# The two gates and the two output projections of a hybrid decoder layer: weights in pairs of K blocks and column blocks, and seven products of block sums for three of eight gate pairs

## The chip, the core and the metric

The kernel runs on one NeuronCore of a Trainium2 chip. Its engines work side by side, each through its own queue in order: TensorE (PE, with its weight loads shown as PEld), VectorE (DVE), ScalarE (ACT), GpSimd (POOL) and SyncE (SP); DMA queues move data between HBM, the on-chip memory SBUF and DRAM scratch. TensorE writes its sums into PSUM, here used as eight banks of 128 x 512 numbers. The metric is the device time of one execution in microseconds, the median of several runs. The changed kernel is timed against the one before on the same chip.

## The reference

One layer on 256 tokens of width 2048, in float32:

```python
h = rmsnorm(x, pre_norm_g)
q_a, c_kv, k_rope, z_mla, c_in, b_gate, c_gate, z_conv, g_mla, g_conv = split(h @ w_in)
attn = causal_mla_attention(...) * silu(z_mla)      # 16 heads, from q_a, c_kv, k_rope
y_mla = attn @ w_o_mla                              # 2048 x 2048
u = c_gate * c_in
conv = sum(conv_w[k] * u_pad[:, k:k + s] for k in range(3))
y_conv = (b_gate * conv * silu(z_conv)) @ w_o_conv  # 2048 x 2048
merged = sigmoid(g_mla) * y_mla + sigmoid(g_conv) * y_conv
out = x + rmsnorm(merged @ w_out, post_norm_g)
```

`g_mla` and `g_conv` are two more products of 256 x 2048 by 2048 x 2048, of the normalised input with columns of `w_in`. These four products and the sum that joins them are called the merged stage here; behind it comes the product with `w_out`.

## The kernel before

**Number format.** Every matrix product is made from three matmuls (`product`, L227): each float32 operand is split into a high and a low part of a format that TensorE takes at full pace, and high x high, high x low and low x high are added up in PSUM. For weights the split is made on the chip: ScalarE copies the float32 piece into the high part (`whi`, L245), and VectorE subtracts it from the piece to get the low part (`wlo`, L246), both in `split_act`. For activations both parts stand side by side in tiles whose names end in `_both`: `x_both` (the input, 16 blocks of K by 256 tokens), `at_both` (the gated attention), `cv_both` (the gated convolution) and `m_both` (the merged result).

**Weights.** All weights come in units of 128 x 2048 numbers (1 MB), in the order of a list called `plan`. `take(i)` hands out unit i; ahead of that, `ahead` has started the loads of the next units (three buffers `raw`) and issued the splits up to unit i + 1. The split halves, of 1024 columns, live in rings of five buffers, `whi` and `wlo`: a half can be split as soon as the matmuls that read the half five places earlier are done. A unit feeds 24 matmuls.

**Stages.** The products for the latents come first, then 16 rounds of attention heads mixed with the convolution's products, then the merged stage, then the output. In the merged stage before, an outer loop runs over four blocks of 512 columns (c), an inner one over the four products (n): gate of the attention, gate of the convolution, attention's projection, convolution's projection. `tokens(c, n, cols)` (L934) makes one of them: four units of four K blocks each, for two groups of 128 tokens (t), into two PSUM banks of the ring "mm" (four banks). The gates go through the sigmoid (L970) into 512-wide tiles `sg`, the projections are multiplied in (L980, L985), the two are added (L986), turned block by block through DRAM (`turned`, L316: VectorE transposes blocks of 32, GpSimd issues four stores and, behind their landing, one load), and split into `m_both` by `features` (L953) some units later. During the first block of columns the attention and the convolution are split into `at_both` and `cv_both` (L924, L929).

**Banks.** PSUM has rings of banks by name: "mm" (four), "cv" (two, for the convolution's products in the attention stage), "st" (one, scores of a head) and "o" (one, values of a head). The values of the last head are read from "o" by L395 on ScalarE and L396 on VectorE.

**Memory.** SBUF is handed out in pools that are opened and closed. The attention stage's pool is `bp`; at its close (L913) the pool of `at_both` and `cv_both` is opened where it was (L914). Among `bp`'s buffers are `mv` and `cw`, through which the last pieces of the convolution are turned at the very end of the attention stage. At L1009 `main` is closed and the pool `op` opened, with the residual `xr`, the weighted output `og` and the post-norm gain `gb` (L1016), which `out_block` (L1019) reads for each output block.

**Order.** The instructions of each engine are put in order by a scheduler that plans with its own estimates of durations: of the instructions that are ready it takes the one that stands first in the program. TensorE's matmuls, and whatever is marked `keep_in_program_order`, stay in program order.

Of the kernel before, what the change touches and what calls it, by code (L numbers as in the profile page):

```python
# [41 lines left out]
XW = S + R  # L42

# [39 lines left out]
def tile_layer(ctx: ExitStack, tc: tile.TileContext, xw, w0, xb, x, pos, pvec, post_g, wc, wz, wcv, wkr, wqk, wqr, wv, cwr, wsq, out):  # L83
# [84 lines left out]
    def split_unit(i):  # L168
# [12 lines left out]
        if i <= u_qa[-1]:  # L181
# [8 lines left out]
            return  # L190
        for h in range(0, w, HALF):
            n = min(HALF, w - h)
            if u_out[3, 0] <= i < u_out[3, 3]:
                hi, lo = (op.tile([P, HALF], F32R, name=f"w{o}{i}_{h}") for o in ("hi", "lo"))
# [5 lines left out]
        splits[i] = parts  # L200

# [11 lines left out]
    def take(i):  # L213
        ahead(i)
        parts = splits.pop(i)

# [700 lines left out]
    dp = main.enter_context(tc.tile_pool(name="dp", bufs=1))  # L917

    def split_turned(src, both, c, t):
        ks, ts = slice(4 * c, 4 * c + 4), slice(t * P, (t + 1) * P)  # L920
        lo = slice(t * P + S, (t + 1) * P + S)
        split_act(quarters(both[:, ks, ts]), quarters(both[:, ks, lo]), by_rows(src, 4), True)

    def split_branch(i):  # L924

        for t in range(NT):
            split_turned(at_t[:, i, t, :], at_both, i, t)

    def split_channels(i):  # L929

        j, t = divmod(i, NT)
        split_turned(cv_t[:, j, t, :], cv_both, j, t)

    def tokens(c, n, cols):  # L934

        pss = [bank(f"sq{c}_{n}_{t}") for t in range(NT)]
        for kk in range(4):
            w = take(u_d[c][n][kk])
            if c == 0 and n == 0:
                split_branch(kk)  # L940
# [253 lines left out]
```

## Time and profile before

| what | value |
|---|---|
| time, median of 3 runs | 1034.92 us (1034.39 to 1035.58) |
| span of the profiled execution | 1033.7 us |
| what lies around the span, against the median | 1.2 us |
| TensorE matmuls, busy | 1027.6 us, 4684 matmuls |
| VectorE busy | 683.5 us, 957 instructions |
| ScalarE busy | 527.4 us, 735 instructions |
| merged stage, first to last matmul | 590.5 to 938.7 us |
| output product | 938.7 to about 1027 us |

The profiled execution has no device time of its own beside its span, so sums are made against the span and carried to the median. Engines overlap, so their busy times don't add up to the span. A matmul's shown duration overlaps those of its neighbours; the pace of a row of them is the stretch divided by their count. In the rows shown below, the first number of a timeline row is its start in us from the span's start, the second its duration; "x8" counts instructions; a bracket gives the idle time in front and what ended it. In rows of groups the numbers behind the bar are busy time in us, mean duration in ns, and the idle time in front.

### The profile page before, as it was taken

How to read it: one execution, taken by the hardware profiler on the slowest of the kernel's cores; microseconds unless marked ns; L12 is line 12 of the kernel's file. 1: busy time of each engine (PE TensorE's matmuls, PEld its weight loads, DVE VectorE, ACT ScalarE, POOL GpSimd, SP SyncE). 2: the span in 40 equal slices, each digit the busy share in tenths (PEclk: the TensorE clock that was granted, in tenths of full speed). 3: DMA queues.
4: the chain of work that ended last, by engine and by line, in shares of the span. 5: the costliest groups of instructions: out<-in, count | busy, mean ns of one | idle time of the engine just before them, and what ended most of it. 6: DMA issues, size and time to landing. Idle time of an engine off the chain costs nothing.

```text
span 1033.7 us, 12740 instructions
## 1 busy us (share of the span) xinstructions
PE 1027.6 (99%) x4684; PEld 856.7 (83%) x4684; DVE 683.5 (66%) x957; ACT 527.4 (51%) x735; POOL 178.7 (17%) x344
## 2 busy tenths in 40 slices
PE   9999999999999999999999999999999999999998
PEld 8888888888888888888888888888888888888886
DVE  7588787787777777777777785564455455455562
ACT  7665545655456454564555565344434444443451
POOL 4540421104300223112133120020010001002000
PEclk9999999999999999999999999999999999999999
DMA  9775865668665676857686765565565557558642
GB/s 353 278 261 204 276 221 219 211 197 288 215 250 193 223 265 209 275 187 242 228 270 226 265 217 199 204 226 185 200 219 209 188 201 241 183 188 337 228 163 81
DMA packets 44526, 233.25 MB, mean 226 GB/s; under 512 B 7952, under 2 KB 10512, under 8 KB 21552
## 3 DMA queue, kind: packets, MB, share of 16 engines
q1 hardware_dynamic: 32400, 199.67, 54.6%
q0 software_dynamic: 11632, 29.48, 8.8%
q10 hardware_dynamic: 432, 3.29, 0.8%
q8 instruction: 36, 0.59, 0.2%
q14 instruction: 26, 0.21, 0.1%
HBM read 215.66 MB, written 12.58 MB: 221 GB/s over the span
## 4 chain that ended last, share of the span: by engine, by line
PE 96%; DMA 2%; ACT 1%; DVE 0%; issue 0%; DVEq 0%; SPq 0%
PE cv L88 34%; PE sq L88 34%; PE out L88 8%; PE z L88 6%; PE qa L88 2%; PE vv L88 2%; PE kn L88 2%; PE qn L88 2%; PE ckv L88 2%; PE sc L88 1%; PE qr L88 1%; PE o L88 1%; DMA raw<-wz_dram 1%; DMA at_f<-far_qa 1%; DMA at_f<-far_ckv 0%
## 5 line engine op out<-in xcount | busy, mean ns | idle before, releaser
L246 DVE TENSOR_TENSOR wlo<-raw,whi 128x1024 fp32r<-128x1024 f32 (+1 forms) x370 | 440.5, 1196 | 279.8 <-ACT whi L245 268.4
L245 ACT ACTIVATE whi<-raw 128x1024 fp32r<-128x1024 f32 (+1 forms) x372 | 382.4, 1035 | 401.6 <-PE sq L88 180.5
L88 PE MATMUL cv<-whi,x_both 128*128 128x512 f32 x1024 | 319.8, 389 | 0.0
L88 PEld LDWEIGHTS cv<-whi,x_both 128*128 128x128 f32 x1024 | 192.3, 188 | 39.4
L88 PE MATMUL cv<-wlo,x_both 128*128 128x512 f32 x512 | 199.6, 390 | 0.0
L88 PE MATMUL sq<-whi,x_both 128*128 128x512 f32 x512 | 158.3, 389 | 0.0
L88 PEld LDWEIGHTS sq<-whi,x_both 128*128 128x128 f32 x512 | 96.1, 188 | 19.9
L88 PEld LDWEIGHTS cv<-wlo,x_both 128*128 128x128 f32 x512 | 96.1, 188 | 19.5 <-DVE wlo L246 0.2
L88 PE MATMUL sq<-wlo,x_both 128*128 128x512 f32 x256 | 99.6, 389 | 0.0
L88 PE MATMUL z<-whi,x_both 128*128 128x512 f32 x256 | 80.0, 389 | 0.0
L88 PE MATMUL sq<-whi,at_both 128*128 128x512 f32 x256 | 79.5, 389 | 0.0
L88 PE MATMUL sq<-whi,cv_both 128*128 128x512 f32 x256 | 79.5, 389 | 0.0
L88 PE MATMUL out<-whi,m_both 128*128 128x512 f32 x256 | 78.9, 389 | 0.0
L328 POOL DMA_DIRECT2D far<-sg x32 | 17.5, 553 | 313.0 <-DVE sg L320 238.4
L328 POOL DMA_DIRECT2D far<-via x64 | 35.1, 556 | 177.9 <-DVE via L320 177.9
L88 PEld LDWEIGHTS sq<-wlo,x_both 128*128 128x128 f32 x256 | 48.0, 188 | 10.0
L88 PEld LDWEIGHTS sq<-whi,at_both 128*128 128x128 f32 x256 | 48.0, 188 | 9.9
L88 PEld LDWEIGHTS out<-whi,m_both 128*128 128x128 f32 x256 | 48.0, 188 | 9.9
L88 PEld LDWEIGHTS sq<-whi,cv_both 128*128 128x128 f32 x256 | 48.0, 188 | 9.9
L88 PEld LDWEIGHTS z<-whi,x_both 128*128 128x128 f32 x256 | 48.1, 188 | 9.9
L88 PE MATMUL z<-wlo,x_both 128*128 128x512 f32 x128 | 49.8, 389 | 0.0
L88 PE MATMUL sq<-wlo,at_both 128*128 128x512 f32 x128 | 49.8, 389 | 0.0
(216 smaller groups left out, 1128.9 us busy)
## 6 DMA issues: line engine op xcount, KB each, us to landing
raw<-wsq_dram SPq DMA_DIRECT2D x80, 1024.0 KB, 4.8
raw<-wcv_dram SPq DMA_DIRECT2D x64, 1024.0 KB, 5.6
raw<-wz_dram SPq DMA_DIRECT2D x16, 1024.0 KB, 4.9
raw<-wqk_dram SPq DMA_DIRECT2D x8, 1024.0 KB, 6.0
cw<-cwr_dram POOLq DMA_DIRECT2D x24, 256.0 KB, 6.0
raw<-wc_dram SPq DMA_DIRECT2D x4, 1024.0 KB, 10.5
raw<-wv_dram SPq DMA_DIRECT2D x4, 1024.0 KB, 4.8
far<-via POOLq DMA_DIRECT2D x64, 48.0 KB, 4.1
```

The lines of the kernel that those rows point to most:

```text
L88: return tc.keep_in_program_order(nc.tensor.matmul(*a, **kw))
L245: a = nc.scalar.activation(hi, src, AF.Copy)
L246: b = nc.vector.tensor_tensor(lo, src, hi.bitcast(F32), op=ALU.subtract)
L328: tc.keep_in_program_order(queue.dma_start(out=f[i], in_=m))
```

## The change

The weights of the four products are now packed in pairs: a unit holds two blocks of K (128 rows each) by two blocks of columns (512 each), that is four blocks b11, b22, b21, b12, for pair k of eight and column block c of two. The loops run over the product n outside and c inside, so a block (n, c) has eight units and four accumulated outputs (two groups of tokens t by two blocks of columns j), instead of four units and two outputs.

For the two gates (n < 2), three of the eight pairs (`FAST`: 0, 3, 5) are not multiplied as eight blocks, but with seven: VectorE forms sums of the four blocks of weights (`split_seven`: three sums, then three and a half splits where two were), once per kernel sums of the four blocks of activations (`mixed`, kept in `mix`), and the seven products go into seven banks (`p1`, `q5`, `q7`, `q6`, `p2`, `q3`, `q4`). The other five pairs add their plain products onto four banks (`p2`, `q3`, `q4`, `d22`), so a block of a gate uses all eight banks: the four "mm", "st", "o" and both "cv". `first_sums` (after the last of the three units) and `last_sums` (at the end of the block) join them into the gate. In the first block the order of the pairs is 1, 2, 0, 4, 3, 6, 5, 7.

The tiles change place: the sums, `mix` and the gates in their full width (`gate`) lie in a new pool `sp`, opened at the close of `bp`; the split attention goes into `x_both`, block by block, behind the last gate's matmuls, the split convolution into the freed `at_f` and `x_both`, the merged result into `x_both`. The merged result is turned in two lots of four pieces instead of four lots of two. The output product begins with the first two units of three column blocks, and splits the last merged pieces ahead of its sixth unit instead of its third; `op` is opened there, after the close of `sp`.

```diff
+PAIRS = KD // 2
+FAST = (0, 3, 5)
...
-    u_d = [[[add(wsq[n, c, k]) for k in range(4)] for n in range(4)] for c in range(4)]
-
-    out_order = [(c, k) for c in range(2) for k in range(3)] + [(0, 3), (1, 3)]
-    out_order += [(c, k) for c in (2, 3) for k in range(4)]
-    u_out = {ck: add(wsq[4, ck[0], ck[1]]) for ck in out_order}
+    pair_order = {(n, c): list(range(PAIRS)) for n in range(4) for c in range(2)}
+    pair_order[0, 0] = [1, 2, 0, 4, 3, 6, 5, 7]
+    u_d, seven = {}, set()
+    for n in range(4):
+        for c in range(2):
+            for k in pair_order[n, c]:
+                u_d[n, c, k] = add(wd[n, c, k])
+                if n < 2 and k in FAST:
+                    seven.add(u_d[n, c, k])
+
+    out_order = [(c, k) for c in range(3) for k in range(2)] + [(c, k) for c in range(3) for k in (2, 3)]
+    out_order += [(3, k) for k in range(4)]
+    u_out = {ck: add(wo[ck[0], ck[1]]) for ck in out_order}
 
...
+        if i in seven:
+            splits[i] = split_seven(i, t)
+            return
...
+    def split_seven(i, t):
+        hi, hi2 = (wpool.tile([P, HALF], F32R, name=f"whi{i}_{j}", tag="whi", bufs=5) for j in range(2))
+        lo, lo2 = (wpool.tile([P, HALF], F32R, name=f"wlo{i}_{j}", tag="wlo", bufs=5) for j in range(2))
+        ta, tb = (sp.tile([P, HALF], F32, name=f"ts{i}_{j}", tag="ts", bufs=2) for j in range(2))
+        ha, hb = (sp.tile([P, HALF], F32R, name=f"th{i}_{j}", tag="th", bufs=2) for j in range(2))
+        la, lb = (sp.tile([P, HALF], F32R, name=f"tl{i}_{j}", tag="tl", bufs=2) for j in range(2))
+        plus = lambda o, a, b: nc.vector.tensor_tensor(o, a, b, op=ALU.add)
+        two = lambda a: a.rearrange("p (j c) -> p j c", j=2)
+        plus(two(ta[:, :]), two(t[:, :HALF]), t[:, 3 * R :].unsqueeze(1).to_broadcast([P, 2, R]))
+        plus(tb[:, :R], ta[:, :R], t[:, R:HALF])
+        plus(tb[:, R:], tb[:, :R], t[:, HALF : 3 * R])
+        split_act(hi[:, :], lo[:, :], t[:, :HALF])
+        split_act(hi2[:, :R], lo2[:, :R], t[:, HALF : 3 * R])
+        split_act(ha[:, :], la[:, :], ta[:, :])
+        split_act(hb[:, :], lb[:, :], tb[:, :])
+        f = lambda a: (a[:, :R], a[:, R:])
+        (b11, b22), (t1, t3), (t2, t4) = (list(zip(f(h), f(l))) for h, l in ((hi, lo), (ha, la), (hb, lb)))
+        return {"b11": b11, "b22": b22, "b21": (hi2[:, :R], lo2[:, :R]), "t1": t1, "t2": t2, "t3": t3, "t4": t4}
 
...
-    fstack = main.enter_context(ExitStack())
-    fp = fstack.enter_context(tc.tile_pool(name="fp", bufs=1, side="right"))
-    at_f = fp.tile([P, H, S], F32, name="at_f")
-    cv_f = fp.tile([P, KD, S], F32, name="cv_f")
+    cstack, astack = (main.enter_context(ExitStack()) for _ in range(2))
+    cv_pool = cstack.enter_context(tc.tile_pool(name="cv_pool", bufs=1, side="right"))
+    cv_f = cv_pool.tile([P, KD, S], F32, name="cv_f")
+    at_pool = astack.enter_context(tc.tile_pool(name="at_pool", bufs=1, side="right"))
+    at_f = at_pool.tile([P, H, S], F32, name="at_f")
...
     bstack.close()
-    cp = main.enter_context(tc.tile_pool(name="cp", bufs=1))
-    at_both = cp.tile([P, H, 2 * S], F32R, name="at_both")
-    cv_both = cp.tile([P, KD, 2 * S], F32R, name="cv_both")
...
-    def tokens(c, n, cols):
-
-        pss = [bank(f"sq{c}_{n}_{t}") for t in range(NT)]
...
+    spool = ctx.enter_context(ExitStack())
+    sp = spool.enter_context(tc.tile_pool(name="sp", bufs=1))
+    gate = [[sp.tile([P, D], F32, name=f"g{n}_{t}") for t in range(NT)] for n in range(2)]
+    mix = {k: sp.tile([P, 2, 4 * P], F32R, name=f"mix{k}") for k in FAST}
+
...
+    def mixed(k):
+        tmp = sp.tile([P, R], F32, name=f"xr{k}", tag="ev", bufs=2)
+        f = tmp[:, :].rearrange("p (j s) -> p j s", j=2)
+        ks = slice(2 * k, 2 * k + 2)
+        nc.vector.tensor_tensor(f, x_both[:, ks, :S].bitcast(F32), x_both[:, ks, S:].bitcast(F32), op=ALU.add)
+        raw = sp.tile([P, R], F32, name=f"xm{k}", tag="ev", bufs=2)
+        a11, a21, a12, a22 = (f[:, j, t * P : (t + 1) * P] for j in range(2) for t in range(2))
+        m7, m5, m6, m3 = (raw[:, j * P : (j + 1) * P] for j in range(4))
+        minus = lambda o, a, b: nc.vector.tensor_tensor(o, a, b, op=ALU.subtract)
+        minus(m7, a21, a11)
+        minus(m5, a21, a22)
+        minus(m6, a11, m5)
+        minus(m3, a12, m6)
+        split_act(mix[k][:, 0, :], mix[k][:, 1, :], raw[:, :])
+
...
+    def fast_block(n, c, part, outs, between):
+        q = {name: bank(f"{name}_{n}{c}") for name in ("p1", "q5", "q7", "q6")}
+        q["p2"] = bank(f"p2_{n}{c}", tag="st", bufs=1)
+        q["q3"] = bank(f"q3_{n}{c}", tag="o", bufs=1)
+        q["q4"], q["d22"] = (bank(f"{name}_{n}{c}", tag="cv", bufs=2) for name in ("q4", "d22"))
+        order = pair_order[n, c]
+        calls = []
+        for k in order:
+            if k in FAST:
+                for name, a, b in (
+                    ("p1", part(2 * k, 0), "b11"), ("q5", mix_part(k, 1), "t1"), ("q7", mix_part(k, 0), "t3"),
+                    ("q6", mix_part(k, 2), "t2"), ("p2", part(2 * k + 1, 0), "b21"), ("q3", mix_part(k, 3), "b22"),
+                    ("q4", part(2 * k + 1, 1), "t4"),
+                ):
+                    calls.append((k, name, a, b))
+            else:
+                for name, t, j in (("p2", 0, 0), ("q3", 0, 1), ("q4", 1, 0), ("d22", 1, 1)):
+                    for i in range(2):
+                        calls.append((k, name, part(2 * k + i, t), {(0, 0): 0, (1, 1): 1, (1, 0): 2, (0, 1): 3}[i, j]))
+        firsts, lasts = {}, {}
+        for at, (k, name, a, b) in enumerate(calls):
+            firsts.setdefault(name, at)
+            lasts[name] = at
+        t_a, t_b = (sp.tile([P, R], F32, name=f"ev{i}_{n}{c}", tag="ev", bufs=2)[:, :] for i in range(2))
+        (o11, o12), (o21, o22) = outs
+        tt = lambda o, a, b, op=ALU.add: nc.vector.tensor_tensor(o, a, b, op=op)
+
+        def first_sums():
+            nc.scalar.activation(t_a, q["p1"][:, :], AF.Copy)
+            tt(t_b, q["q6"][:, :], t_a, ALU.subtract)
+            tt(o12, q["q5"][:, :], t_b)
+            tt(o21, q["q7"][:, :], t_b)
+            tt(o22, q["q5"][:, :], o21)
+
+        def last_sums():
+            tt(o11, q["p2"][:, :], t_a)
+            tt(o12, q["q3"][:, :], o12)
+            tt(o21, q["q4"][:, :], o21, ALU.subtract)
+            tt(o22, q["d22"][:, :], o22)
+
+        at = 0
+        for i, k in enumerate(order):
+            w = take(u_d[n, c, k])
+            if i == order.index(max(FAST)) + 1:
+                first_sums()
+            between(i)
+            while at < len(calls) and calls[at][0] == k:
+                _, name, a, b = calls[at]
+                product(q[name][:, :], a, w[b] if k in FAST else w(b, R), firsts[name] == at, lasts[name] == at)
+                at += 1
+        last_sums()
+
...
+    for n in range(2):
+        for c in range(2):
+
+            def between(i):
+                if n == c == 0 and i < 2:
+                    for k in FAST[i : i + 1] if i == 0 else FAST[1:]:
+                        mixed(k)
+                if n == c == 1 and i in (2, 4, 6):
+                    split_group(at_place, at_t, i // 2 - 1)
+
+            outs = [[gate[n][t][:, columns(c, j)] for j in range(2)] for t in range(NT)]
+            fast_block(n, c, x_part, outs, between)
             for t in range(NT):
+                for o in outs[t]:
+                    nc.scalar.activation(o, o, AF.Sigmoid, scale=r_col[:, t : t + 1])
+    def between(c, i):
+        if (c, i) == (0, 1):
+            split_group(at_place, at_t, 3)
+        elif (c, i) == (0, 3):
+            astack.close()
+            cv_first["area"] = cv_stack.enter_context(tc.tile_pool(name="cv_first", bufs=1, side="right")).tile(
+                [P, KD // 2, 2 * S], F32R, name="cv_first"
+            )
+        if (c, i) in ((0, 4), (0, 6), (1, 3), (1, 5)):
+            split_group(cv_place, cv_t, {(0, 4): 0, (0, 6): 1, (1, 3): 2, (1, 5): 3}[c, i])
+
+    for c in range(2):
+        q = plain_block(2, c, x_part, lambda i: between(c, i))
+        for (t, j), ps in q.items():
+            g = gate[0][t][:, columns(c, j)]
+            nc.vector.tensor_tensor(g, ps[:, :], g, op=ALU.mult)
+    for c in range(2):
+        q = plain_block(3, c, cv_part, lambda i: features(i - 4) if c and i in (4, 5) else None)
         steps = []
+        for (t, j), ps in q.items():
+            m, y = (gate[i][t][:, columns(c, j)] for i in range(2))
+            nc.vector.tensor_tensor(y, ps[:, :], y, op=ALU.mult)
+            nc.vector.tensor_tensor(m, m, y, op=ALU.add)
+            steps.append((turned(m, y, 4), m))
+            steps[-1][0][0]()
+        for (_, come), m in steps:
+            come(m)
+
...
+    for i, (c, kk) in enumerate(out_order[:6]):
         w = take(u_out[c, kk])
-        if i == 2:
-            features(3, waiting, m_both)
+        if i == 5:
+            for j in (2, 3):
+                features(j)
         out_products(pss[c], w, kk)
-    main.close()
-
+    spool.close()
+    cv_stack.close()
+    cstack.close()
+    op_w = ctx.enter_context(tc.tile_pool(name="op_w", bufs=1, side="right"))
```

`plain_block` is the same loop for the two projections, with eight products per unit into four banks ("mm" for c = 0; "st", "o", "cv", "cv" for c = 1).

More of the change, by code (lines that the diff above doesn't have):

```diff
@@ new lines, in plain_block @@
+    def plain_block(n, c, part, between):
+        tags = ("mm",) * 4 if c == 0 else ("st", "o", "cv", "cv")
+        q = {
+            (t, j): bank(f"sq{n}{c}_{t}{j}", tag=tag, bufs={"mm": 4, "cv": 2}.get(tag, 1))
+            for (t, j), tag in zip(((0, 0), (0, 1), (1, 0), (1, 1)), tags)
+        }
+        order = pair_order[n, c]
+        for at, k in enumerate(order):
+            w = take(u_d[n, c, k])
+            between(at)
+            for (t, j), ps in q.items():
+                for i in range(2):
+                    b = w({(0, 0): 0, (1, 1): 1, (1, 0): 2, (0, 1): 3}[i, j], R)
+                    product(ps[:, :], part(2 * k + i, t), b, at == i == 0, at == PAIRS - 1 and i == 1)
+        return q
@@ L1082, in finish_by_two @@
         store(t, 1024, 1280, o[:, 512:])
-    for c, kk in out_order[3:6]:
-        out_products(pss[c], take(u_out[c, kk]), kk)
     for c in range(3):
-        if c == 2:
-            pss.append([bank(f"out{c}_{t}") for t in range(NT)])
-        for kk in range(4) if c == 2 else (3,):
+        for kk in (2, 3):
             out_products(pss[c], take(u_out[c, kk]), kk)
```

109 lines of the change are left out of this document (40 added, 69 removed).

## The prediction

> **What bounds the kernel now.** I read the page's head and its chain of waits first, then that chain in order of time, then what TensorE waited for, then the busy times in stretches of the merged stage.
>
> ```profile
> span 1033.7 us, 12740 instructions
> PE 1027.6 (99%) x4684; PEld 856.7 (83%) x4684; DVE 683.5 (66%) x957; ACT 527.4 (51%) x735; POOL 178.7 (17%) x344
> ...
> PE 96%; DMA 2%; ACT 1%; DVE 0%; issue 0%; DVEq 0%; SPq 0%
> ```
>
> ```profile
> 590.51 348.20 PE sq L88 x1536
> ```
>
> ```profile
> PE idle L88 <- PEq L1182: 0.8, 1, 0.8
> PE fin L88 <- ACT dg L1069: 0.4, 1, 0.4
> PE vv L88 <- DVE f L396: 0.2, 1, 0.2
> ```
>
> ```profile
> core 0: us, PE busy (x) PEld busy (x) DVE busy (x) ACT busy (x) POOL busy (x), PEclk, DMA share, GB/s
> 590.50:612.30 21.80, 21.80 (x98) 18.02 (x97) 17.45 (x24) 12.08 (x18) 5.50 (x10) 1.00 0.67 241
> 677.50:720.90 43.40, 43.40 (x193) 35.96 (x192) 22.42 (x22) 19.87 (x21) 5.49 (x10) 1.00 0.63 218
> 590.50:938.70 348.20, 348.20 (x1538) 288.29 (x1537) 192.77 (x190) 156.43 (x168) 22.22 (x41) 1.00 0.59 206
> ```
>
> TensorE sets the end: 96% of the chain, 1.4 us of waiting in all, and in the merged stage (the "sq" products) 1536 matmuls in one piece of 348.20 us. That is 348.20/1536 = 0.2267 us for each, which I use below; the duration of 389 ns that a single one shows overlaps its neighbours. A unit (1 MB of weights, 24 matmuls) is 5.44 us. VectorE is busy 22.4 us of each 43.4 in the steady stage, half. At the stage's start it is busy 17.45 of 21.8, since the attention stage's last work still stands on it. The span is 1033.7 us and the median of the runs 1034.92, so 1.2 us lie around the span; I add every difference to the median.
>
> **What is removed.** Twelve of the gates' 32 units (three of eight in each of four blocks) use seven block products instead of eight: 12 x 3 = 36 matmuls fewer (4648 in all), 36 x 0.2267 = **8.2 us**. Nothing else on TensorE changes in number, and as it never waits today, 8.2 us is the most that can be gained. Each remaining matmul still loads its own weights, and no bytes of weights are added or dropped.
>
> **What is added on VectorE.** Rows that price it, in order of time, from the last stage into this one:
>
> ```profile
> 590.85 0.74 DVE L751 SCALAR_TENSOR_TENSOR cg<-cv,r_both,cg 128x512 f32<-128x512 f32 x1
> 591.64 1.23 DVE L246 TENSOR_TENSOR wlo<-raw,whi 128x1024 fp32r<-128x1024 f32 x1
> 592.78 0.68 DVE L752 TENSOR_TENSOR cv_w<-cv_w,cg 128x512 f32<-128x512 f32 x1
> 593.38 0.69 DVE L785 TENSOR_TENSOR cv_f<-cv_f,cw 128x512 f32<-128x512 f32 x1
> 593.99 0.42 DVE L396 TENSOR_TENSOR f<-o,half 128x256 f32<-128x256 f32 x1
> 594.32 0.68 DVE L756 TENSOR_TENSOR cv_f<-cv_f,cv_w 128x512 f32<-128x512 f32 x1
> 594.92 0.68 DVE L785 TENSOR_TENSOR cv_f<-cv_f,mv 128x512 f32<-128x512 f32 x1
> 595.52 0.42 DVE L693 TENSOR_TENSOR at_f<-f,at_f 128x256 f32<-128x256 f32 x1
> 595.86 0.70 DVE L320 STREAM_TRANSPOSE cw<-cv_f 128x512 f32<-128x512 f32 x1
> 596.49 1.18 DVE L246 TENSOR_TENSOR wlo<-raw,whi 128x1024 fp32r<-128x1024 f32 x1
> 597.59 0.68 DVE L756 TENSOR_TENSOR cv_f<-cv_f,cv_w 128x512 f32<-128x512 f32 x1
> 598.19 1.22 DVE L246 TENSOR_TENSOR wlo<-raw,whi 128x1024 fp32r<-128x1024 f32 x1
> 599.32 0.70 DVE L320 STREAM_TRANSPOSE mv<-cv_f 128x512 f32<-128x512 f32 x1
> ```
>
> ```profile
> L648 DVE TENSOR_TENSOR p<-p,mask 128x128 f32<-128x128 f32 x16 | 4.5, 280 | 0.0
> ```
>
> The starts of neighbours lie closer than their durations: 592.78 to 593.38 is 0.60 us for 512 columns (duration 0.68), 598.19 to 599.32 is 1.13 for 1024 (duration 1.22). In a full queue the distance counts: 0.60, 1.13, and for 128 columns 0.28 less the same 0.08, 0.20. A plain unit costs 2 x 1.13 = 2.3 us. A unit of seven has three sums (1.13 + 2 x 0.60), three splits of 1024 and one of 512 (3 x 1.13 + 0.60): 6.3 us. A block of eight units, with its eight sums out of PSUM (8 x 0.60), is 3 x 6.3 + 5 x 2.26 + 4.8 = **35.0 us**, against TensorE's 183 x 0.2267 = 41.5. By durations (1.22, 0.69) it is 38.6, still below. So blocks two to four are covered: the ring of five half-units lets the splits run about one and a half units ahead, and a late unit is caught up within two plain ones.
>
> [...]
>
> **The first block, where it is decided.** VectorE holds there, beside 35 us, the ten left-overs above (all rows but the three splits, about 5.8 us) and the three `mixed` (each 0.60 + 4 x 0.20 + 0.60 = 2.0), some 47 us in 41.5. Two waits come ahead of that sum.
>
> First, the bank "o". The new block takes all eight banks, `q3` that of the last head's values. Its second group of six matmuls, due at 590.34 + 6 x 0.2267 = 591.7, writes the bank that L396 reads at 593.99 to 594.41. TensorE waits 2.7 us; all its later matmuls stand behind. Unit one ends at 598.5, unit two at 603.9, and `p1`, the first three matmuls of the first unit of seven, at 604.6 (without any wait: 601.9). Today the first product writes "mm" banks and needs nothing of the attention.
>
> Second, the memory. `mix`, the sums and their splits lie in the pool `sp`, opened where the attention's pool `bp` closes. How such a pool waits is seen twice:
>
> ```profile
> 594.73 1.06 ACT L245 ACTIVATE whi<-raw 128x1024 fp32r<-128x1024 f32 x1 [2.84 <-PE sq L88]
> ...
> 607.87 4.26 ACT L245 ACTIVATE at_both<-at_f 128x512 fp32r<-128x512 f32 x8
> ```
>
> ```profile
> 600.32 2.17 POOL L328 DMA_DIRECT2D far<-mv  x4 [1.26 <-DVE mv L320]
> 603.90 0.57 POOL L332 DMA_DIRECT2D cv_f<-far  x1 [1.42 <-DMA far<-mv]
> 605.06 0.57 POOL L332 DMA_DIRECT2D cv_f<-far  x1 [0.58 <-DMA far<-mv]
> ```
>
> ```profile
> 938.75 0.34 ACTq L1016 DMA_DIRECT2D gb<-post_g_dram  x1
> ```
>
> ```profile
> L88 PE MATMUL sq<-whi,at_both x256: 389/389/389, 633.9 to 916.6; 128*128 128x512 f32 x128
> ...
> L88 PE MATMUL sq<-whi,cv_both x256: 389/389/389, 655.7 to 938.3; 128*128 128x512 f32 x128
> ```
>
> Of `at_both`'s eight splits six have had their sources for long, and ACT was idle 2.84 us before 594.73; yet all eight start at 607.87, after the last `bp` buffer, `mv`, was carried off (landed at 605.06, when the load behind it goes). And `gb`, 32 KB into its pool (behind `xr` and `og`) and so over `at_both`, goes at 938.75, when the neighbour `cv_both` was last read, and not after 916.6. A new pool waits for the whole old one. (ACT itself has room: by these rows 3.5 instead of 2 splits of 1.06 us in three units of a block, five more readings of PSUM at 4.26/8 = 0.53 or little more, some 25 us of 41.5.) So nothing of `sp` can be written before about 605.1; or down to 602.8, if the two splits at 596.49 and 598.19 move behind the last transpose, as the later release of the ring in unit one suggests. I take 604.0.
>
> From there `q5` needs of VectorE: the sum and four differences (0.60 + 0.80, some 0.3 for their chain), the wide sum 1.13, the split of `mix` 0.60, by the order of the program also the two half sums (1.3 with their chain), and the split of the sum 1.13: 5.9 us, at least 4.6 without the half sums. `q5` starts at **609.9** (607.4 to 611.2). TensorE stood idle since 604.6; counted from 601.9 the first block has lost 8.0 us, the bank's 2.7 among them (5.5 to 9.3).
>
> After it: VectorE ends the unit at 611.0, half a plain unit (1.13; the other half fits in ahead of 604) and two `mixed` at 616.1, and the second unit of seven (6.3, but for its last split) at 621.3. TensorE leaves the first at 609.9 + 18 x 0.2267 = 614.0, the plain unit at 619.4, and has its `q5` at 620.1: 1.2 us late. The third is ready at 629.9 and needed at 631.5. The next block's first is split at 639.5, the sums of the old block behind it are done at 642.2, and they hold the bank that `q5` would write at 641.7: 0.5. I take these 1.7 us; the bounds are 0, if the order within the queue is kinder, and 4, nearly what durations give in the second rival. In all 9.7 us lost (5.5 to 13.3) against 8.2 gained: **1034.9 - 8.2 + 9.7 = 1036.4 us**, its own range 1032.2 to 1040.0.
>
> **What costs nothing.** The new `at`, `cv` and merged splits go into `x_both` and the freed `at_f`; they are as many as before, and stand on VectorE in blocks with 20 us spare. Four turned pieces instead of two come back at once: 16 + 4 issues on POOL at 0.55 and two landings, about 20 us after a block, and are split behind 21.8 us (four units) or 27.2 (five). If that cover were gone, ACT and VectorE would hold the weight splits behind them, and TensorE would lose what goes beyond the lead of 8 us. One more pool stands ahead of a load:
>
> ```profile
> gb<-post_g_dram ACTq DMA_DIRECT2D x1, 1024.0 KB, 5.0
> ```
>
> `gb` now waits for `sp`, whose last reader is the split ahead of the sixth output unit, about 30 us into the output; it is read after eight units, at 43.5, and takes 5.
>
> **Rivals.** (1) *The pool does not hold back, the work is early.* Only the bank (2.7) and the ledger remain: left-overs, first unit of seven and its `mixed` end at 590.85 + 5.8 + 6.3 + 2.0 = 604.9, in time for a late TensorE; two `mixed` and the next plain unit reach 611.2 against 608.7, the next of seven 617.5: some 5 us lost, **1031.7**. For it: the idle VectorE between splits; against: both rows on pools. Chance 0.22. (2) *VectorE's queue becomes the bound through the first block* (the other side). If operations cost their durations, since each waits for ACT or for the one in front, `q5` starts at 610.3, the second unit of seven is 1.8 us late, the sums at the block's end (3.2 + 2.75 us behind 642.3) hold the banks of the next block another 3: 13.4 lost, **1040.1**. It decides from a loss of 8.2 on. For it: 17.45 of 21.8 us already taken; against: the 0.60 rows. Chance 0.20. (3) *TensorE comes back slow from its idle 5.3 us.* The trace has one start:
>
> ```profile
> 4.56 1.78 PE L88 MATMUL qa<-whi,x_both 128*128 128x512 f32 x4
> ...
> 6.63 1.07 PE L88 MATMUL qa<-whi,x_both 128*128 128x512 f32 x4
> ```
>
> The first four took 1.78 where four take 1.07, 0.7 us, though data may have been late too. One to three such lots give 0.7 to 2.1 more, **1037.7**; chance 0.10. [...] That fewer products are not in fact issued has no ground in the code. Remaining chance for the forecast: 0.48.
>
> **How the numbers follow.** A measurement here can tell about 0.2%, 2.1 us: faster is below 1032.8, slower above 1037.0. The forecast's 0.48 divides into 0.04 faster, 0.33 same, 0.11 slower; rival 1 into 0.20 and 0.02 same; rival 2 is slower; rival 3 0.02 same and 0.08 slower. Sum: faster 0.24, same 0.37, slower 0.39. The range 1031.0 to 1040.5 holds the forecast, rival 3, most of rival 2 and half of rival 1.
>
> **What would show it.** Matmuls 4648; TensorE waiting some 2.7 us for L396 just after 591.7, then some 5 us for the splits of the first sums, little after 645. Wrong: first sums well before 602 (rival 1), waits of TensorE on VectorE in blocks two to four (rival 2), matmul starts wider than 0.23 us after the gap (rival 3).

## The result and the profile after

The changed kernel takes 1042.87 us (median of 4 runs, 1042.44 to 1043.13), the kernel before 1035.24 us on the same chip (1034.39 to 1035.58): a ratio of 1.0076, 95% interval 1.0062 to 1.009. It is slower by 7.6 us. The forecast was 1036.4 with a range up to 1040.5, so it missed on the slow side. The spans of the two profiled executions differ by 7.4 us.

The page's head, its row of the granted clock and its chain, then what TensorE waited for:

```profile
span 1041.1 us, 12831 instructions
...
PE 1022.9 (98%) x4648; PEld 851.5 (82%) x4648; DVE 752.3 (72%) x1067; ACT 546.5 (52%) x766; POOL 179.8 (17%) x344
...
PEclk9999999999999999999999979999999999999999
```

```profile
PE q L90 <- issue: 7.8, 1, 7.8
PE q L90 <- DVE f L432: 2.6, 1, 2.6
PE q L90 <- DVE mix L281: 1.6, 1, 1.6
PE idle L90 <- PEq L1312: 0.8, 1, 0.8
```

The 36 matmuls are gone (4648). Three new waits of one occurrence each have come, and one slice of the clock row is at 7. (Line numbers are those of the changed kernel: L90 is a matmul, L280 and L281 the high and the low split, L222 the sums of weights, L988 and L992 `mixed`, L432 the old L396, L1034 the copy of p1 in `first_sums`, L1031 its sums.) TensorE's timeline puts all of it in the first 30 us of the merged stage:

```profile
594.21 0.50 PE L90 MATMUL q<-whi,x_both 128*128 128x512 f32 x1 [2.57 <-DVE f L432]
...
612.49 0.77 PE L90 MATMUL q<-th,mix 128*128 128x512 f32 x1 [7.78 <-issue]
...
615.25 1.22 PE L90 MATMUL q<-th,mix 128*128 128x512 f32 x2 [1.57 <-DVE mix L281]
...
620.11 0.60 PE L90 MATMUL q<-wlo,mix 128*128 128x512 f32 x1
620.54 0.41 PE L90 MATMUL q<-whi,mix 128*128 128x512 f32 x1
```

Busy times in stretches of the same execution (columns as in the prediction; the clock is the first number behind POOL's):

```profile
607.00:612.00 5.00, 0.00 (x0) 0.00 (x0) 5.00 (x10) 2.36 (x3) 0.00 (x0) 0.50 0.62 213
612.00:617.00 5.00, 2.94 (x6) 1.96 (x7) 5.00 (x9) 0.39 (x1) 0.00 (x0) 0.50 0.46 190
617.00:620.50 3.50, 3.50 (x9) 2.67 (x9) 2.99 (x6) 2.15 (x3) 0.00 (x0) 0.50 0.00 0
620.50:625.00 4.50, 4.50 (x21) 3.66 (x20) 4.50 (x8) 2.71 (x4) 0.00 (x0) 0.99 0.31 78
...
678.00:722.00 44.00, 44.00 (x196) 36.44 (x195) 38.74 (x42) 25.91 (x29) 0.00 (x0) 1.00 0.57 207
```

From 612.49 to 620.54 TensorE does 14 matmuls in 8.05 us. Without the 1.57 us wait that is 6.48 where 14 x 0.2267 is 3.17: 3.3 us lost at the granted clock 0.50. So 2.57 + 7.78 + 1.57 + 3.3 = 15.2 us are lost and 8.2 gained, +7.0; 0.4 of the 7.4 I can't place. The steady block (678 to 722) is as the prediction had it: TensorE full, VectorE at 38.7 of 44.

Why the first q5 starts at 612.49 is in VectorE's queue, with ScalarE's row for the copies that VectorE waits for and POOL's row for the landing of `mv`:

```profile
604.48 2.36 DVE L281 TENSOR_TENSOR wlo<-raw,whi 128x1024 fp32r<-128x1024 f32 x2 [3.53 <-ACT whi L280]
606.75 0.69 DVE L988 TENSOR_TENSOR xr<-x_both 128x512 f32<-128x512 f32 x1
607.36 1.22 DVE L222 TENSOR_TENSOR ts<-raw 128x1024 f32<-128x1024 f32 x1
...
612.78 1.22 DVE L222 TENSOR_TENSOR ts<-raw 128x1024 f32<-128x1024 f32 x1
...
614.51 0.69 DVE L281 TENSOR_TENSOR mix<-xm,mix 128x512 fp32r<-128x512 f32 x1
```

```profile
603.38 2.01 ACT L280 ACTIVATE whi<-raw 128x1024 fp32r<-128x1024 f32 x2 [3.69 <-PE d L90]
```

```profile
602.64 0.57 POOL L368 DMA_DIRECT2D cv_f<-far  x1 [1.10 <-DMA far<-mv]
```

`mv` has been carried off at 602.6, but the first sum starts only at 606.75: the planned order has two splits in front of it, of weights that are used only later. VectorE stands idle for 3.53 us ahead of them, since their copies on ScalarE wait until 603.38 for halves of the ring that TensorE must first set free. TensorE itself is late by 2.57. Then, at 612.78, the next unit's sums go ahead of the low part of `mix`, which the third matmul of q5 wants.

### The profile page after: what moved, and what is told of

Same layout as the page of the kernel before. It is cut to its first block, busy times and chain, and to the rows that moved or that the text cites. A ratio compares the mean times of both kernels' runs of the same rounds, so it can differ in the third digit from the quotient of the medians.

```text
span 1041.1 us, 12831 instructions
## 1 busy us (share of the span) xinstructions
PE 1022.9 (98%) x4648; PEld 851.5 (82%) x4648; DVE 752.3 (72%) x1067; ACT 546.5 (52%) x766; POOL 179.8 (17%) x344
## 4 chain that ended last, share of the span: by engine, by line
PE 97%; DVE 1%; ACT 0%; DMA 0%; issue 0%; DVEq 0%
PE cv L90 34%; PE sq L90 17%; PE q L90 9%; PE z L90 8%; PE out L90 8%; PE p L90 4%; PE d L90 3%; PE qa L90 2%; PE kn L90 2%; PE qn L90 2%; PE vv L90 2%; PE ckv L90 2%; PE sc L90 1%; PE qr L90 1%; PE o L90 1%; PE kr L90 0%
## 5 line engine op out<-in xcount | busy, mean ns | idle before, releaser
L281 DVE TENSOR_TENSOR wlo<-raw,whi 128x1024 fp32r<-128x1024 f32 (+1 forms) x370 | 431.2, 1178 | 205.3 <-ACT whi L280 198.1
L280 ACT ACTIVATE whi<-raw 128x1024 fp32r<-128x1024 f32 (+1 forms) x372 | 373.1, 1020 | 375.7 <-PE cv L90 115.3
L90 PE MATMUL cv<-whi,x_both 128*128 128x512 f32 x1024 | 319.8, 389 | 0.0
L90 PEld LDWEIGHTS cv<-whi,x_both 128*128 128x128 f32 x1024 | 192.3, 188 | 39.5
L90 PE MATMUL cv<-wlo,x_both 128*128 128x512 f32 x512 | 199.5, 390 | 0.0
L90 PE MATMUL sq<-whi,x_both 128*128 128x512 f32 x384 | 118.7, 389 | 0.0
L90 PEld LDWEIGHTS cv<-wlo,x_both 128*128 128x128 f32 x512 | 96.1, 188 | 19.3
L90 PEld LDWEIGHTS sq<-whi,x_both 128*128 128x128 f32 x384 | 72.1, 188 | 15.0
L90 PE MATMUL z<-whi,x_both 128*128 128x512 f32 x256 | 80.0, 389 | 0.0
L90 PE MATMUL out<-whi,x_both 128*128 128x512 f32 x256 | 79.0, 389 | 0.0
L90 PE MATMUL sq<-wlo,x_both 128*128 128x512 f32 x192 | 74.7, 389 | 0.0
L90 PEld LDWEIGHTS out<-whi,x_both 128*128 128x128 f32 x256 | 48.0, 188 | 10.1
L90 PEld LDWEIGHTS z<-whi,x_both 128*128 128x128 f32 x256 | 48.1, 188 | 9.9
L90 PE MATMUL q<-whi,x_both 128*128 128x512 f32 x160 | 52.6, 390 | 2.6 <-DVE f L432 2.6
L90 PE MATMUL z<-wlo,x_both 128*128 128x512 f32 x128 | 49.8, 389 | 0.0
L90 PE MATMUL out<-wlo,x_both 128*128 128x512 f32 x128 | 49.8, 389 | 0.0
L90 PE MATMUL p<-whi,x_both 128*128 128x512 f32 x128 | 47.0, 393 | 0.0
L90 PEld LDWEIGHTS sq<-wlo,x_both 128*128 128x128 f32 x192 | 36.0, 188 | 7.5
L364 POOL DMA_DIRECT2D far<-cw x48 | 26.2, 553 | 78.6 <-DVE cw L356 78.6
L90 PE MATMUL sq<-whi,cv_first 128*128 128x512 f32 x128 | 39.7, 389 | 0.0
```

Source lines behind the costliest of these rows:

```text
L90: return tc.keep_in_program_order(nc.tensor.matmul(*a, **kw))
L280: a = nc.scalar.activation(hi, src, AF.Copy)
L281: b = nc.vector.tensor_tensor(lo, src, hi.bitcast(F32), op=ALU.subtract)
L364: tc.keep_in_program_order(queue.dma_start(out=f[i], in_=m))
```

## The experiments

The expectations call the kernels by short names; each stands behind the heading of its experiment.

**1. The new packing without the seven products (e_plain).** All gate pairs are eight block products in pairs, in their natural order; no sums, no `mixed`, and four banks for a block instead of eight, so that the bank "o" is not wanted at the start.

```diff
-                if n < 2 and k in FAST:
+                if False:
...
-            fast_block(n, c, x_part, outs, between)
+            for (t, j), ps in plain_block(n, c, x_part, between).items():
```

> All eight pairs of the gates are multiplied as eight blocks (no sums, no mix); the pairing, the new places of the tiles, the two lots of four turned pieces and the later output pools stay. Theory: the loss of the changed kernel lies in the first block's seven products alone, so this is the time of before, 1035 us within 1 us, 4684 matmuls, and TensorE waits under 2 us in all. Rival: the new places and pools cost by themselves; then it is 1037 us or more with waits after 780 us.

Measured: 1035.52 us against 1035.17, ratio 1.0005 (0.9996 to 1.0015). TensorE waits 0.8, 0.4 and 0.4 us in all, none of them in the merged stage. The new pairing, places, pieces and `gb` cost nothing that can be measured; all of the loss belongs to the seven products, with their sums, `mixed` and the banks that they take.

**2. Does the clock fall because TensorE stands idle? (e_warm)** First 32 matmuls, whose sum is thrown away, ahead of the first q5.

```diff
+                if (n, c, k, name) == (0, 0, FAST[0], "q5"):
+                    for j in range(32):
+                        matmul(q[name][:, :], x_both[:, 0, :P], x_both[:, j % KD, :], start=True, stop=True)
```

> The changed kernel with 32 matmuls that serve nothing, into the bank of q5 just before its first product in the first unit of seven, where TensorE stood idle for 7.8 us; their sum is overwritten. Theory: after that idle time TensorE ran at a granted clock of 0.50 until about 620.5, some 18 matmuls at 0.43 us instead of 0.23, 3.5 us; kept busy it stays at 1.00 and the time is 1039.4 us, though 32 matmuls more are run. Rival: the wide spacing after the gap is VectorE's work arriving late, not the clock; then the time stays at 1042.9 us.

Measured: 1042.84 us, ratio 1.0081 (1.0056 to 1.0106), no gain. But the clock fell in this execution elsewhere, after the two gaps that the dummies did not cover. Its TensorE rows and stretches:

```profile
594.29 0.80 PE L90 MATMUL q<-whi,x_both 128*128 128x512 f32 x1 [2.57 <-DVE f L432]
...
616.69 0.73 PE L90 MATMUL q<-th,mix 128*128 128x512 f32 x2 [2.06 <-DVE mix L281]
```

```profile
594.20:597.00 2.80, 2.71 (x6) 2.17 (x7) 2.77 (x6) 0.00 (x0) 0.31 (x1) 0.50 0.23 91
...
618.00:621.00 3.00, 3.00 (x8) 2.35 (x8) 2.93 (x6) 2.01 (x3) 0.00 (x0) 0.50 0.00 0
```

So this run could not decide the question as it was put: it covered 7.4 us and left 2.57 and 2.06 open. Its four executions speak for the clock all the same: they took 1041.31, 1042.31, 1043.37 and 1047.43 us, in the order of their mean granted clock (0.999, 0.998, 0.996 and 0.993). The question was asked again in experiment 5.

**3. The bank wait alone (e_bank).** In plain pairs q3 comes last instead of second, so the "o" bank is wanted 2.7 us later.

```diff
-                for name, t, j in (("p2", 0, 0), ("q3", 0, 1), ("q4", 1, 0), ("d22", 1, 1)):
+                for name, t, j in (("p2", 0, 0), ("q4", 1, 0), ("d22", 1, 1), ("q3", 0, 1)):
```

> In plain units of the gates the products go p2, q4, d22, q3 instead of p2, q3, q4, d22, so the bank of the last head's values is written last, after it was read. Theory A: the first sums are held by the landing of the last turned piece (about 602.6 us) and the order planned behind it, a fixed time; the 2.6 us wait at 591 goes, and comes back in the wait for q5: 1042.9 us within 0.7. Theory B: the first sums stand in VectorE's queue behind a split that waits for TensorE to free a half-unit; then all of it moves ahead by 2.6 us: 1040.3 us.

Measured: 1039.69 us, ratio 1.0043 (1.0028 to 1.0058), 3.2 us better than the changed kernel. The 2.57 us are gone, and the other two waits keep their lengths (7.8 and 1.6). VectorE's rows:

```profile
601.58 2.36 DVE L281 TENSOR_TENSOR wlo<-raw,whi 128x1024 fp32r<-128x1024 f32 x2 [2.51 <-ACT whi L280]
603.86 0.68 DVE L988 TENSOR_TENSOR xr<-x_both 128x512 f32<-128x512 f32 x1
```

The sums came 2.9 us earlier too, again right behind the two splits. A TensorE that is late at the bank frees its ring late, so VectorE is late with the sums: the bank's wait and the wait for the sums add up, and do not overlap.

**4. Does the old pool hold the sums back? (e_land)** As experiment 3, with the four stores that turn the last piece of `mv` issued twice, so that its landing comes later.

```diff
-        go()
+        [go() for _ in range(2 if (j, t) == (3, 0) else 1)]
```

> The bank order of e_bank; the four stores that turn the last piece of `mv` are issued twice, so that its landing, the last reader of the old pool, comes about 2.2 us later (near 605.4 instead of 603.2). Theory B (the first sums stand in VectorE's planned order behind two splits, and the landing of `mv` is past by then): the first sum stays near 603.9, and the time at 1039.7 (1039.0 to 1040.5). Theory A (the new pool waits for the landing, as the prediction took it): the first sum not before 605.4, the wait ahead of q5 9.3 us or more, and 1041.5 (1041.0 to 1042.5).

Measured: 1044.35 us, ratio 1.0085 (1.0071 to 1.0099). VectorE and POOL of this kernel:

```profile
601.91 2.36 DVE L281 TENSOR_TENSOR wlo<-raw,whi 128x1024 fp32r<-128x1024 f32 x2 [2.55 <-ACT whi L280]
608.96 0.69 DVE L988 TENSOR_TENSOR xr<-x_both 128x512 f32<-128x512 f32 x1 [4.70 <-DMA cv_f<-far]
```

```profile
609.12 0.56 POOL L368 DMA_DIRECT2D cv_f<-far  x1 [4.24 <-DMA far<-mv]
```

The splits in front are as early as in experiment 3, yet the sums wait 4.70 us and start with the landing of `mv`, behind which POOL's load goes at 609.12. (The bracket names another transfer of the same turning; POOL's row names that of `mv`.) The landing moved by about 6 us, not by the 2.2 expected (why the doubled stores took so long is not shown); the time moved by 4.7, so both lie beyond what theory A expected, on its side. So the pool's rule holds: the first sum starts at the later of two points, the landing of `mv` and the end of the splits planned ahead of it. In the changed kernel it was the second, in experiment 3 the two are 0.7 us apart (landing 603.19).

**5. The clock, with everything covered (e_warm2).** Experiment 3's order and 43 dummy matmuls.

> The bank order of e_bank, and 43 matmuls on `x_both` into q5's bank ahead of the first q5, whose sum is thrown away (the real q5 starts its bank anew): 43 x 0.2267 = 9.7 us, which covers the 7.8 us wait and the 1.6 us wait behind it. Theory (the clock halves because TensorE is idle): the granted clock stays 1.00 through 595 to 625, no matmul of the real work is 0.43 apart, and the time is that of e_bank less the 3 us that its slow matmuls cost: 1036.7 (1035.5 to 1038.0), with TensorE waiting no longer than 0.5 us. Rival (the clock falls for another cause, or the slow matmuls hide behind VectorE anyway): 1039.7 or more, since the dummy work can only be in the way.

Measured: 1037.17 us, ratio 1.002 (1.001 to 1.0029), 2.5 us faster than experiment 3 though it issues 43 matmuls more. TensorE and its clock:

```profile
602.28 9.91 PE L90 MATMUL q<-x_both 128*128 128x512 f32 x43
...
612.99 0.73 PE L90 MATMUL q<-th,mix 128*128 128x512 f32 x2 [0.35 <-DVE mix L281]
```

```profile
605.00:612.00 7.00, 7.00 (x32) 5.82 (x31) 7.00 (x12) 2.76 (x3) 0.00 (x0) 1.00 0.82 312
612.00:617.00 5.00, 4.65 (x21) 3.50 (x20) 4.93 (x11) 2.73 (x4) 0.00 (x0) 1.00 0.05 21
```

The clock stays at 1.00 and no real matmul is 0.43 apart. That is the idle's second price, shown: the standing still itself costs 7.8 + 1.6 us, the half clock behind it another 2.5 to 3.

**6. The sums later in the first block (e_late).** Its pairs in the order 1, 2, 4, 6, 0, 3, 5, 7, so that four plain units come ahead of the first unit of seven.

```diff
-    pair_order[0, 0] = [1, 2, 0, 4, 3, 6, 5, 7]
+    pair_order[0, 0] = [1, 2, 4, 6, 0, 3, 5, 7]
```

> The first block takes its pairs in the order 1, 2, 4, 6, 0, 3, 5, 7: four plain units first, then the three of seven. Theory: the loss was the start of the new pool's work, not VectorE's amount; with two units more in front, only the bank's 2.6 us and up to 2 us for three units of seven in a row remain, the clock stays at 1.00: 1035.2 - 8.2 + 2.6 to 4.6 = 1029.6 to 1031.6 us. Rival: VectorE has more work in the first block than fits (some 47 us in 41.5); then 5 us or more of waits remain, spread over the first block and the start of the second: 1033 us or more.

Measured: 1040.91 us, ratio 1.0058 (1.0041 to 1.0075). Its waits, and VectorE in the 20 us behind the change of pools:

```profile
PE q L90 <- ACT mix L280: 3.8, 1, 3.8
PE q L90 <- DVE f L432: 2.6, 1, 2.6
PE q L90 <- DVE tl L281: 1.7, 1, 1.7
PE q L90 <- DVE mix L281: 1.4, 2, 1.0
```

```profile
605.00:625.00 20.00, 15.76 (x69) 12.39 (x67) 20.00 (x30) 10.17 (x13) 0.56 (x1) 0.98 0.47 173
```

The 7.8 became 3.8, but beside it and the bank's 2.6 stand three more waits (1.7, and twice for `mix`, 1.4), and VectorE is full without a gap in these 20 us. Behind it the granted clock fell here too (0.50 from 624.33 to 631.16). This is what the rival of this run expected, VectorE's amount of work in the block; that the order in its queue adds to it was not tested.

**7 to 9. Only part of the first block with seven products (e_one, e_one2, e_two).** With the bank order of experiment 3: first pair 5 alone, put second to last; then pair 5 alone in its natural place, `mixed` earlier; then pairs 3 and 5.

```diff
-                if n < 2 and k in FAST:
+                if n < 2 and k in (FAST if n + c else FAST[2:]):
...
-                if n == c == 0 and i < 2:
-                    for k in FAST[i : i + 1] if i == 0 else FAST[1:]:
-                        mixed(k)
+                if n == c == 0 and i in (3, 5, 6):
+                    mixed(FAST[{3: 2, 5: 0, 6: 1}[i]])
```

In the second of them `mixed` comes at i = 2, 3, 4; in the third `FAST[1:]` stands for `FAST[2:]` and `mixed` comes at i = 1, 3, 4.

> The bank order of the second version (plain units take p2, q4, d22, q3) and, in the first block, only the pair 5 with seven products, as the second to last of the block; the other two `mixed` still in this block; 30 matmuls fewer than before. Theory (the loss in the first block is the nearness of the block sums to the change of pools, not the sums themselves): no wait above 1 us at the change, 30 x 0.2267 = 6.8 us come through: 1028.4 (1027.3 to 1030.0), that is 0.7 below the version with a plain first block. Rival (any block sums in the first block stop VectorE, which has the turning of `mv` there): a wait of 1 us or more ahead of the first q5 of this pair, and not faster than the version with a plain first block: 1029.1 or more.

> In the first block only pair 5 with seven products, the pairs in their natural order, so that two plain pairs come behind it; the three `mixed` at the third, fourth and fifth pair, so that their two `ev` buffers are free again before the block's own first sums want them; the other blocks as in the changed kernel; bank order of e_bank. 30 matmuls fewer than before. Theory (in e_one the two waits of 2.5 and 2.3 us at the end of the first block came from `ev`: the third `mixed` held the two buffers that p1's copy needs): no TensorE wait above 1 us behind the first 10 us, clock 1.00, 30 x 0.2267 = 6.8 us come through: 1028.5 (1027.5 to 1029.5). Rival (VectorE's amount: the first block with one such pair, three `mixed` and the sums for the next block is still too full): a wait of 1 us or more at the end of the first block or ahead of q5, a granted clock below 1.00, and 1031 or more.

> As e_one2, with pairs 3 and 5 of the first block as seven products; `mixed` for pair 3 at the second pair, for pair 5 at the fourth, for pair 0 of the next block at the fifth. 33 matmuls fewer than before. Theory (what decides is the distance from the change of pools: VectorE has 5.5 us idle of the ten between 600 and 610 where the first block is plain there): the sums of pair 3 are wanted near 611 and start near 604, 7 us for some 6 us of work; no wait above 1 us, 33 x 0.2267 = 7.5 us come through: 1027.8 (1026.8 to 1029.0). Rival (VectorE's amount in this block): waits ahead of q5 or at the block's end of 1 to 4 us, granted clock below 1.00 for 3 to 8 us, and 1030 to 1037.

Measured: 1036.74 (ratio 1.001, 1.0001 to 1.0019), 1037.18 (1.002, 1.0011 to 1.0029) and 1037.96 (1.0025, 1.0016 to 1.0035). All three expectations of a gain fell. The first waited 2.5 and 2.3 us at the end of the block, where its third `mixed` and the copy of p1 want the same two `ev` buffers; moving the three `mixed` forward did not cure it. The granted clock fell to 0.50 in all three, for 10.24, 6.83 and 6.83 us, which adds to the waits. In the second kernel, these are ScalarE and TensorE at the end of the first block:

```profile
632.70 1.06 ACT L280 ACTIVATE whi<-raw 128x1024 fp32r<-128x1024 f32 x1 [2.91 <-PE q L90]
633.67 0.61 ACT L280 ACTIVATE mix<-xm 128x512 fp32r<-128x512 f32 x1
634.19 0.58 ACT L1034 ACTIVATE ev<-p 128x512 f32<-128x512 f32 x1
```

```profile
634.82 0.50 PE L90 MATMUL p<-whi,x_both 128*128 128x512 f32 x1 [1.53 <-ACT ev L1034]
639.75 0.80 PE L90 MATMUL q<-th,mix 128*128 128x512 f32 x1 [3.97 <-DVE ev L1031]
```

The third `mixed`, issued at the fifth pair, reached its split only at 633.67: in front of it on ScalarE stands a split of weights that waits until 632.70 for TensorE to free a half of the ring, as the splits in front of the first sum do in the changed kernel. The copy of p1 goes into the same two `ev` buffers and follows it at 634.19; the next block's p1 and q5 want the banks that this copy and the sums behind it must read first. VectorE was busy without a break from 610 to 630, but not from 630 to 634 (2.43 of 4 us). In the third kernel the first sum starts at 603.53, in the moment of `mv`'s landing, but q5 waits 6.4 us all the same, since splits of weights come between the sums:

```profile
603.53 0.69 DVE L988 TENSOR_TENSOR xr<-x_both 128x512 f32<-128x512 f32 x1 [0.51 <-DMA far<-mv]
...
606.56 1.23 DVE L281 TENSOR_TENSOR wlo<-raw,whi 128x1024 fp32r<-128x1024 f32 x1 [0.79 <-ACT whi L280]
```

(The third expectation counted on 5.5 us of idle VectorE between 600 and 610; it is 5.3 in the kernel of experiment 1 and 4.3 in that of experiment 10.) So neither the place alone nor one buffer explains it. One unit of seven in this block, together with the three `mixed` and the sums for the next block, was in these orders enough to make TensorE wait; how much of that is VectorE's amount of work and how much the order of the queues is not shown.

**10. The first block plain, the others with seven products (e_three).**

```diff
-                if n < 2 and k in FAST:
+                if n < 2 and (n, c) != (0, 0) and k in FAST:
...
-                if n == c == 0 and i < 2:
-                    for k in FAST[i : i + 1] if i == 0 else FAST[1:]:
-                        mixed(k)
+                if n == c == 0 and i in (3, 4, 5):
+                    mixed(FAST[i - 3])
...
+            if n == c == 0:
+                for (t, j), ps in plain_block(n, c, x_part, between).items():
```

The sigmoid of these four outputs reads PSUM directly, and the pairs of this block stand in their natural order.

> The first block (the first half of the first gate) is computed as eight block products in every pair, as in the version without block sums; the three `mixed` for the later blocks are made in the first block, at its fourth, fifth and sixth pair, and the other three blocks keep their seven products. 27 matmuls fewer than before. Theory (the block sums cost nothing from the second block on; all that is lost is lost in the first block, at the change of pools and banks): no TensorE wait above 1 us behind the first 10 us, granted clock 1.00, and the 27 x 0.2267 = 6.1 us come through whole: 1029.1 (1028.0 to 1030.5). Rival (the later blocks lose something too, which the first block's delay hides, for instance VectorE's load of 35 us in blocks of 43): waits in blocks two to four, 1031.5 or more. Rival (a program that gives the clock an easier load, or a harder one): the same waits, another clock.

Measured: 1029.18 us (1028.72 to 1029.89), ratio 0.994 (0.9926 to 0.9954): faster than both kernels, and all of the 27 x 0.2267 = 6.1 us came through. Its waits and its four gate blocks:

```profile
PE idle L90 <- PEq L1315: 0.8, 1, 0.8
PE fin L90 <- ACT dg L1203: 0.4, 1, 0.4
```

```profile
594.00:638.00 44.00, 44.00 (x196) 36.43 (x195) 34.48 (x48) 24.04 (x28) 5.50 (x10) 1.00 0.58 198
638.00:680.00 42.00, 42.00 (x187) 34.80 (x186) 35.37 (x39) 24.35 (x28) 0.00 (x0) 1.00 0.54 199
680.00:722.00 42.00, 42.00 (x187) 34.80 (x186) 36.98 (x41) 24.71 (x28) 0.00 (x0) 1.00 0.59 206
722.00:764.00 42.00, 42.00 (x187) 34.78 (x186) 33.93 (x39) 24.10 (x30) 0.00 (x0) 1.00 0.60 218
```

TensorE is full in each, at the clock 1.00. VectorE is at 33.9 to 37.0 us per block, in the later ones near the 35.0 of the prediction's sum by start distances.

## Why the prediction was wrong, by its own steps

**The gain: right.** 4648 matmuls, 8.2 us, and experiment 10 has the price of one to within the spread of its runs (6.1 us worked out, 6.3 between experiments 1 and 10).

**VectorE's sums from block two on, and what costs nothing: right.** No new wait of TensorE lies behind 616 us, and neighbours on VectorE start 0.61 us apart for 512 columns (606.75 to 607.36), as the distances of before had it; experiment 1 shows the new places to be free.

**The bank "o": right in size, wrong in how it adds.** 2.7 was said, 2.57 measured. The prediction took the landing at an absolute time, so that the bank's wait was swallowed ("8.0 us, the bank's 2.7 among them"). But what stands in front of the sums waits for TensorE, so the 2.57 move the sums along. Experiment 3 gets back 3.2 us where the prediction's way of adding would have given nothing. This is the first step that failed.

**The start of the first sums: the same step, from its other side.** "I take 604.0", with bounds of 602.8 to 605.1; measured 606.75. The mechanism that set these bounds is real (experiment 4, and experiment 9's sum that starts with the landing), and `mv` was gone by 602.6, as the lower bound had it. But it was not the last condition: the step asked when the memory is free and not what the planned order has in front on the same queue, though it had itself seen that two splits "move behind the last transpose". From the sum to q5 5.9 us were predicted; 612.49 - 606.75 = 5.74 were measured. Counted as there, 2.57 + 7.78 = 10.35 us were lost up to q5, and not 8.0. With the bank's wait away (experiment 3) the first sum starts at 603.86 and q5 at 609.59, beside the forecast's 604.0 and 609.9: its 604.0 came out there by luck, since the splits in front ended 0.7 us behind the landing, the only condition it had named.

**The residual of 1.7 us: right in size by chance, wrong in place.** The ledger had it at the second unit of seven and at the end of the block. Neither made TensorE wait; 1.57 us came inside the first unit, at the low part of `mix`, which stands behind the next unit's sums.

**The clock: the second step that failed, a term that was given as a rival.** Rival 3 had the mechanism, at 0.7 to 2.1 us and a chance of 0.10; measured are 3.3 us in the changed kernel, and 2.5 us come back when the idle is filled (experiment 5). With TensorE idle for 5.3 us in the forecast itself, the row of the slow start should have made this a term of the sum. The price was set too low because only the first lots after the idle were counted: the clock stayed at 0.50 for 8 us after work began again at 612.49, with another wait, of 1.57 us, among its first matmuls (whether that wait prolonged it is not shown). That less than 3.3 comes back is as it should be: the third matmul of q5 waits for the low part of `mix` until 615.25 at any clock, and from there the 12 matmuls up to 620.54 took 5.29 us instead of 2.72, 2.6 more.

**The other rivals.** Rival 1 (nothing holds the work back) fell: sums at 606.75. Rival 2 named 1040.1 through VectorE's amount of work in the first block. In the changed kernel that is not where the time went. With the sums moved away from the change of pools VectorE is full in experiment 6, as this rival has it; in experiments 7 to 9 its part and that of the order were not separated. None of the four other places for the sums that were tried made the first block free; that none exists is not shown.

Forecast and result, from 8.2 gained: 9.7 lost as 8.0 and 1.7 in the forecast; 15.2 lost as 10.35, 1.57 and 3.3 in the trace.

## What to carry to other kernels

When new work opens a stage, write down for its first operation every condition: the memory, the banks, and what the queue's order puts in front of it; if one of these itself waits for the engine that you hope to relieve, the delays add, as the bank's 2.57 us and the 7.78 us ahead of q5 did here. Price an idle stretch of TensorE of several us twice, once for the idle and once for the half clock behind it: in the changed kernel the wait of 7.78 us was followed by 8 us of work and waiting at 0.50, in which 3.3 us were lost. And try the change where the engine with the added work has room, which here meant leaving out one block of four: 6.3 us gained instead of 7.6 lost.

## What the runs showed of the hardware that was not expected

The clock also fell at much shorter pauses than the 7.8 us wait, but not at each of them. These are the pause of 2.57 us at the bank and the work behind it, in the changed kernel, then in the first kernel with dummies (columns as in the prediction):

```profile
591.60:594.20 2.60, 0.04 (x1) 0.00 (x0) 2.60 (x5) 0.03 (x1) 0.00 (x0) 1.00 0.91 315
594.20:597.00 2.80, 2.79 (x12) 2.33 (x13) 2.77 (x6) 0.00 (x0) 0.40 (x1) 1.00 0.22 88
```

```profile
591.60:594.20 2.60, 0.13 (x1) 0.00 (x0) 2.60 (x5) 0.11 (x1) 0.00 (x0) 0.92 0.90 312
594.20:597.00 2.80, 2.71 (x6) 2.17 (x7) 2.77 (x6) 0.00 (x0) 0.31 (x1) 0.50 0.23 91
```

Behind the same pause the clock is 1.00 in the one (12 matmuls in 2.8 us) and 0.50 in the other (6). A pause of 2.06 us in the first kernel with dummies (0.50 from 618 to 621) and one of 2.48 us in the first kernel of experiments 7 to 9 (0.50 from 635.5 to 645) were followed by 0.50 as well.

The time at half clock differs too: 13.65 us in the changed kernel, from 606.9, 2.2 us into the wait of 7.78 us, to 620.55; 10.24 and twice 6.83 us in experiments 7 to 9; about 3.4 us at each of the two falls in the first kernel with dummies. What decides whether a pause costs the clock, and for how long, is not shown by these runs.
